# Biases loaded as rows, two weight slices in buffers of their own, two input tiles normalized early: a hybrid streaming-encoder layer on one core

## The chip, the cores and the metric

The kernel runs on 1 core of a Trainium2 chip. Its time is the device time of one launch in microseconds, the median over runs of the same build. A separate launch under the hardware profiler gives the trace; the trace's span is the time from the first to the last instruction of the core.

TensorE (PE) multiplies and transposes, VectorE (DVE), ScalarE (ACT) and GpSimd (POOL) work on tiles, SyncE (SP) issues the DMAs. TensorE's two granted clock levels are 1.2 and 2.4 GHz; the profile writes them as 0.5 and 1.0.

## The reference, cut to what matters

```
h = layer_norm(x, ln_in_g, ln_in_b)                     # x: 1024 x 1024
proj = h @ w_in + b_in                                  # 16 column groups
ya = gMLP spatial gating; yb = chunked band attention
yc = indexer (relu scores of iq, ik, iw), top-256 keys, attention over them
km, vm = split(mem @ w_mem_kv, 2)                       # mem: 256 x 1024, w_mem_kv: 1024 x 512
ym = attention of mq over km, vm
mixed = concat(ya*silu(a_g), yb*silu(b_g), yc*silu(c_g), ym*silu(m_g))
out = layer_norm(2**0.25 * h + mixed @ w_out + b_out, ln_g, ln_b)
```

All inputs and the output are float32. The change touches the loads and the order of work ahead of and in the first projections: layer_norm(x), the two biases ln_in_b and b_in, and mem @ w_mem_kv.

## The kernel before, in words

Sequence rows come in 8 tiles of 128 (`NB`); the model width is 8 blocks of 128 (`KT`). The input x is loaded as 8 tiles xt of 128 rows by 1024. `x_rows` normalizes one tile where it lies: two bn_stats, one bn_aggr and one subtract-and-multiply by g_in on VectorE, two tiny steps (add epsilon, power -0.5) on GpSimd (lines 134 and 135), one scaling by rs on ScalarE. The GpSimd and ScalarE steps carry a raised priority (`BOOST`).

`x_parts(half, ...)` turns four tiles: for each of the 8 column blocks TensorE makes 4 transposes into one PSUM bank (xT), ScalarE adds the bias column b_col and writes the high part hTh in a shortened format, VectorE writes what is left as hTl. So hT holds the normalized input, columns of the model on partitions, in two halves of 512 rows, each as a high and a low part.

`wblock` loads one slice of 128 columns of a weight matrix as one DMA into a raw buffer (there are 2, tag "raw"), and splits it in two pieces: ScalarE copies the high part, GpSimd (line 208) subtracts for the low part, into wblk tiles (tag "w", 5 buffers). `project` runs 24 matmuls a slice: for each of 8 blocks high times high, high times low, low times high. One projection of a narrow slice (72 columns: indexer key and indexer weights) has its parts in tiles named wnar; its slice is `wik`. `wmg` is the slice of the first memory gate. mem is turned by `mem_parts` into mT; `kv_of_mem` projects it with four slices of w_mem into km (slices 1 and 2) and vm (slices 3 and 4).

The order in the program is: x tiles 0 to 3, g_in, mem and two w_mem slices by `FIRST_LOADS`; the bias loads; mem turned; x tiles 0 to 3 normalized; km projected, with the loads of w_mem slices 3 and 4 in between (they take over the raw buffers of slices 1 and 2); x's first half turned; vm projected; wik and wmg loaded; the loads of x's tiles 4 to 7, on SyncE behind the fourth w_mem load (`loads[3]`); the first half of the wnar projection; tiles 4 to 7 normalized, on VectorE behind the last hTl of the first half (`first_half[0]`); the first half of the wmg projection; the second half turned; then the rest.

The program order is a priority: a planner with estimated durations and landing times decides the order in which each engine gets its instructions, and which buffer a tile takes. On the chip every engine runs its instructions in that order, each waiting for its inputs, so an instruction that waits holds back all behind it on its engine.

The biases are used as columns, one number a partition: b_col (8 columns) from ln_in_b, bias (31 columns, one for each 128-column group of the projection) from b_in, and hbias, half of bias. They are loaded with the partition as the fast index:

```
SP.dma_start(out=b_col, in_=ln_in_b.rearrange("(t p) -> p t", p=P))
SP.dma_start(out=bias[:m, a:a + n], in_=b_in[c0:c0 + n * m].rearrange("(t p) -> p t", p=m))
```

so each element is a piece of its own, 1024 in the first and 26 x 128 + 72 + 4 x 128 = 3912 in the three of bias.

Of the kernel before, what the change touches and what calls it, by code (L numbers as in the profile page):

```python
# [11 lines left out]
F32 = mybir.dt.float32  # L12
# [7 lines left out]
ALU = mybir.AluOpType  # L20
# [4 lines left out]
P = 128  # L25
NB = 8
KT = 8
# [46 lines left out]
def f32(ap):  # L74
    return ap.bitcast(F32)
# [3 lines left out]
def tile_trunk(ctx, tc, x, mem, ln_in_g, ln_in_b, w_in, b_in, a_ln_g, a_ln_b, a_ws, a_bs,  # L79
               b_rel_rev, t5_table, w_mem, w_out, b_out, ln_g, ln_b, bucket1h, out):  # L80
    nc = tc.nc
    G, SP = nc.gpsimd, nc.sync
# [20 lines left out]
    PE, V, S = Engine(nc.tensor), Engine(nc.vector), Engine(nc.scalar)  # L103

    def run(steps):

        while True:
            try:
                next(steps)
            except StopIteration as e:  # L110
                return e.value

    cp = ctx.enter_context(tc.tile_pool(name="cp", bufs=1))
    gp = ctx.enter_context(tc.tile_pool(name="gp", bufs=1))
# [4 lines left out]
    ident = cp.tile([P, P], F32, name="ident")  # L119
# [8 lines left out]
    def bcast(t, vec):  # L128
        n = vec.shape[-1]
        SP.dma_start(out=t, in_=bass.AP(tensor=vec.tensor, offset=vec.offset, ap=[[0, P], [1, n]]))  # L130
# [5 lines left out]


    col = {}
    bias = cp.tile([P, 31], F32, name="bias")
    hbias = cp.tile([P, 31], F32, name="hbias")  # L140
    spans = ((0, 26, P), (I_K, 1, 72), (M_Q, 4, P))
    for c0, n, _ in spans:
# [1 line left out]
            col[c0 + t * P] = len(col)  # L144

    def load_biases():
        V.memset(hbias, 0.0)
        for c0, n, m in spans:
            a = col[c0]
            SP.dma_start(out=bias[:m, a:a + n], in_=b_in[c0:c0 + n * m].rearrange("(t p) -> p t", p=m))  # L150
            V.tensor_scalar(hbias[:m, a:a + n], bias[:m, a:a + n], 0.5, None, ALU.mult)

    h_dram = [dp.tile([P, DM], F32, name=f"h_dram{r}") for r in range(NB)]

# [15 lines left out]
    def s4(name, dt=F32R, shape=(P, SEQ)):  # L170
        return gp.tile(list(shape), dt, tag="s4", bufs=S4, name=name)
# [11 lines left out]
    E = ep.enter_context(tc.tile_pool(name="ep", bufs=1))  # L183

    def ev(name, bufs=EV):
        return E.tile([P, 512], F32, tag="ev", bufs=bufs, name=name)

    def bank(tag, name=None):
        return ps.tile([P, 512], F32, tag=tag, bufs=BANKS[tag], name=name or tag)


    loads = []

    def wblock(w, c0, m=P):

        raw = E.tile([P, KT, P], F32, tag="raw", bufs=2, name="raw")
        loads.append(SP.dma_start(out=raw[:, :, :m], in_=w[:, c0:c0 + m].rearrange("(k p) c -> p k c", p=P)).ins)
        ts = []
        if m < P:
            narrow = [gp.tile([P, 2, KT // 2, m], F32R, tag=tag, bufs=1, name="wnar") for tag in ("planes", "score6")]  # L200
        for q in range(2):
            t = E.tile([P, 2, 4, P], F32R, tag="w", bufs=WB, name="wblk") if m == P else narrow[q]
            r = raw[:, 4 * q:4 * q + 4, :m]
            if WH[0] <= len(loads) < WH[1]:
                G.tensor_scalar(t[:, 0], r, 1.0, 0.0, ALU.mult, ALU.add)
            else:
                S.activation(t[:, 0], r, AF.Copy)
            G.tensor_sub(t[:, 1], r, f32(t[:, 0]))  # L208
            ts.append(t)
        return ts  # L210

    def project(t, a, b, m=P, hi=hh, lo=hl, tag="pp"):

        acc = bank(tag, "acc")
        for k in range(KT):
            wh, wl = t[k // 4][:, 0, k % 4, :m], t[k // 4][:, 1, k % 4, :m]
            PE.matmul(acc[:m, :b - a], wh, hi(k, a, b), start=(k == 0), stop=False)
            PE.matmul(acc[:m, :b - a], wh, lo(k, a, b), start=False, stop=False)
            PE.matmul(acc[:m, :b - a], wl, hi(k, a, b), start=False, stop=(k == KT - 1))
            yield  # L220
        return acc
# [56 lines left out]


    g_in = s4("g_in", F32)  # L280
    b_col = cp.tile([P, KT], F32, name="b_col")
    mT = [s4(f"mT{i}", F32R, (P, 4, 256)) for i in range(4)]

    def x_load(rb):
        tag = ("S", "S", "S", "S", "s4", "score7", "v3", "v3")[rb]
        xt = gp.tile([P, DM], F32, tag=tag, bufs={"S": SB, "v3": 2, "s4": S4}.get(tag, 1), name="xt")
        SP.dma_start(out=xt, in_=x[rb * P:(rb + 1) * P, :])
        return xt

    def x_rows(rb, xt):  # L290

        st = E.tile([P, 2, 6], F32, tag="st", bufs=2, name="st")
        V.bn_stats(st[:, 0], xt[:, :512])
        V.bn_stats(st[:, 1], xt[:, 512:])
        mv = E.tile([P, 2], F32, tag="mv", bufs=2, name="mv")
        V.bn_aggr(mv, st)
        rs = E.tile([P, 1], F32, tag="rs", bufs=2, name="rs")
        with tc.high_priority(offset=BOOST):
            rstd_of(mv[:, 1:2], rs)
        V.scalar_tensor_tensor(xt, xt, mv[:, 0:1], g_in, ALU.subtract, ALU.mult)  # L300
        with tc.high_priority(offset=BOOST):
            S.activation(xt, xt, AF.Copy, scale=rs)

    def x_parts(half, xts):

        high, rest = hT[half]
        for k in range(KT):
            pt = bank(("pt", "qk")[k % 2], "xT")
            for j in range(4):
                PE.transpose(pt[:, j * P:(j + 1) * P], xts[j][:, k * P:(k + 1) * P], ident)  # L310
            begin = S.activation(high[:, k, :], pt, AF.Identity, bias=b_col[:, k:k + 1])
            end = V.scalar_tensor_tensor(rest[:, k, :], pt, b_col[:, k:k + 1], f32(high[:, k, :]), ALU.add, ALU.subtract)
        return end.ins, begin.ins
# [6 lines left out]
    def mem_parts(r, mt):  # L320
        for q in range(2):
            pt = bank("pt")
            for j in range(4):
                k = 4 * q + j
                PE.transpose(pt[:, j * P:(j + 1) * P], mt[:, k * P:(k + 1) * P], ident)
            src, dst = pt.rearrange("p (a b) -> p a b", a=4), slice(r * P, (r + 1) * P)
            S.activation(mT[q][:, :, dst], src, AF.Copy)
            V.tensor_sub(mT[2 + q][:, :, dst], src, f32(mT[q][:, :, dst]))
# [29 lines left out]
    xts, mts, w_kv = [], [], []  # L358
    for what in FIRST_LOADS:
        if what == "x":  # L360
            xts.append(x_load(len(xts)))
        if what == "m":
            mts.append(mem_load(len(mts)))
        if what == "w":
            w_kv.append(wblock(w_mem, len(w_kv) * P))
        if what == "g":
            bcast(g_in, ln_in_g)
    SP.dma_start(out=b_col, in_=ln_in_b.rearrange("(t p) -> p t", p=P))
    load_biases()
    for r in range(2):  # L370
        mem_parts(r, mts[r])
    for rb in range(4):
        x_rows(rb, xts[rb])
    def kv_of_mem(i):

        t = ev("kv")
        for pair in range(2):
            acc = run(project(w_kv[2 * i + pair], 0, 256, P, mhi, mlo))
            S.activation(t[:, pair * 256:pair * 256 + 256], acc[:, :256], AF.Copy)
            if not i:  # L380
                w_kv.append(wblock(w_mem, 256 + pair * P))
        return t

    km = kv_of_mem(0)
    first_half = x_parts(0, xts)
    vm = kv_of_mem(1)


    wik = wblock(w_in, I_K, 72)
    wmg = wblock(w_in, M_G)  # L390
    ikh = s4("ikh")
# [3 lines left out]
    def ik_half(a, b):  # L395
        acc = run(project(wik, a, b, 72))
        bk = col[I_K]
        with tc.high_priority(offset=BOOST):
            for lo in (0, 64):
                S.activation(ikh[lo:lo + 64, a:b], acc[0:64, :], AF.Identity, bias=bias[0:64, bk:bk + 1])  # L400
            S.activation(iwT[64:72, a:b], acc[64:72, :], AF.Identity, bias=bias[64:72, bk:bk + 1])
            for lo in (0, 64):
                V.scalar_tensor_tensor(ikl[lo:lo + 64, a:b], acc[0:64, :], bias[0:64, bk:bk + 1],
                                       f32(ikh[0:64, a:b]), ALU.add, ALU.subtract)

    with tc.issue_after(loads[3]):
        xts += [x_load(rb) for rb in range(4, NB)]
    ik_half(0, 512)
    with tc.issue_after(first_half[0]):
        for rb in range(4, NB):  # L410
            x_rows(rb, xts[rb])
    run(gate_half(wmg, M_G, 6, 0, "pv"))
    second_half = x_parts(1, xts[4:])
# [390 lines left out]
    for g in range(4):  # L804
        SP.dma_start(out=bsT[64 * (g % 2):64 * (g % 2) + 64, g // 2, :],
                     in_=bass.AP(tensor=a_bs.tensor, offset=a_bs.offset + g * P, ap=[[0, 64], [1, P]]))
# [182 lines left out]
    for i, rb in enumerate(RBS):  # L989
        n = (rb + 1) * P  # L990
# [85 lines left out]
    for i, rb in enumerate(RBS):  # L1076
        n = (rb + 1) * P
# [241 lines left out]
    for k in range(KT):  # L1319
        hi, lo = [t[:, k % 4, :] for t in wo[k // 4]]  # L1320
        raw = E.tile([P, DM], F32, tag="raw", bufs=2, name="rawo")
        SP.dma_start(out=raw, in_=w_out[k * P:(k + 1) * P, :])
        for half in range(2):
            c = slice(half * 512, half * 512 + 512)
# [73 lines left out]
```

## Time and profile before

| | us |
|---|---|
| median of 3 runs | 672.88 (672.48 to 673.44) |
| profiled execution, device time | 671.02 |
| its span | 669.2 |
| TensorE busy | 633.7 (95%) |
| VectorE busy | 477.7 (71%) |
| ScalarE busy | 423.8 (63%) |
| GpSimd busy | 351.8 (53%) |

The mean granted TensorE clock over the span is 0.989. Busy times are sums over the whole span; an engine that is busy for a small share can still hold up another at one place. The chain that ended last is 68% TensorE; the first 50 us hold 13.7 us in which TensorE does not work (36.29 busy of 50), most of them before its first matmuls.

### The profile page before, as it was taken

What the parts mean: (1) busy time and instruction counts of PE and PEld (TensorE: products, weight loads), DVE (VectorE), ACT (ScalarE), POOL (GpSimd) and SP (SyncE); (2) the same over time, 40 slices, a digit from 0 to 9 for tenths busy, and PEclk for the clock granted to TensorE, in tenths of its full rate; (3) what the DMA queues carried; (4) which work ended last, traced back from release to release, by engine and by line L of the source; (5) the groups of instructions that cost most, each with busy time, mean ns of one, the idle gap of its engine ahead of it and who ended that gap; (6) DMA issues with size and microseconds to landing.
All of it is one profiled execution on the core that took longest, in us unless ns stands there. A gap on an engine that the chain in (4) does not pass through costs nothing.

```text
span 669.2 us, 11083 instructions
## 1 busy us (share of the span) xinstructions
PE 633.7 (95%) x3698; PEld 483.0 (72%) x3698; DVE 477.7 (71%) x1165; ACT 423.8 (63%) x947; POOL 351.8 (53%) x354
## 2 busy tenths in 40 slices
PE   4989999999999998988999999799999999999995
PEld 3867877767777777766677767577777777778785
DVE  6684254688866898898988889648658458877535
ACT  4665245576699888858999884446446666346210
POOL 3671320306346796574465645953224756557851
PEclk9999999999999999999999999899999999999998
DMA  9792511102234545255475534463102474225111
GB/s 283 239 328 84 169 54 28 35 18 81 62 111 111 126 119 133 51 129 134 109 131 107 147 83 85 96 136 110 38 12 83 141 247 132 90 82 188 64 63 64
DMA packets 121669, 75.30 MB, mean 113 GB/s; under 512 B 58976, under 2 KB 111500, under 8 KB 121612
## 3 DMA queue, kind: packets, MB, share of 16 engines
q1 hardware_dynamic: 121612, 74.59, 40.6%
q8 instruction: 29, 0.48, 0.3%
q14 instruction: 28, 0.23, 0.1%
HBM read 46.44 MB, written 17.64 MB: 96 GB/s over the span
## 4 chain that ended last, share of the span: by engine, by line
PE 68%; DVE 10%; ACT 9%; POOL 5%; issue 4%; DMA 2%; SPq 0%; POOLq 0%; DVEq 0%; ACTq 0%
PE acc L94 51%; PE qk L94 8%; PE pv L94 5%; ACT jka L94 4%; PE pt L94 3%; DVE jk L94 2%; ACT sc L94 1%; DMA xt<-in_x 1%; POOL wblk L208 1%; DMA pT<-sc 1%; DVE sc L94 1%; POOL rs L134 1%; POOL sc L546 1%; POOL sc L545 1%; PE xT L94 1%
## 5 line engine op out<-in xcount | busy, mean ns | idle before, releaser
L94 PE MATMUL acc<-hTh,wblk 128*128 128x512 f32 (+1 forms) x960 | 323.2, 401 | 2.2 <-ACT hTh L94 1.3
L94 PEld LDWEIGHTS acc<-hTh,wblk 128*128 128x128 f32 x960 | 178.3, 189 | 49.1 <-issue 8.9
L94 PE MATMUL acc<-hTl,wblk 128*128 128x512 f32 (+1 forms) x480 | 188.2, 392 | 0.0
L208 POOL TENSOR_TENSOR wblk<-raw,wblk 128x512 fp32r<-128x512 f32 x72 | 96.5, 1345 | 122.8 <-ACT wblk L94 119.9
L94 PEld LDWEIGHTS acc<-hTl,wblk 128*128 128x128 f32 x480 | 90.7, 189 | 17.6 <-issue 2.2
L94 ACT ACTIVATE jka<-score,cand 128x768 int8<-128x768 f32 (+2 forms) x93 | 96.5, 1038 | 8.7 <-DVE cand L94 8.1
L94 PEld LDWEIGHTS <-pT 128*128 128x128 f16 x656 | 46.2, 99 | 32.5 <-issue 21.7
L546 POOL TENSOR_TENSOR sc<-sc 128x512 f16<-128x512 f32 (+4 forms) x48 | 58.7, 1229 | 2.7
L94 PE MATMUL pv<-v,pT 128*128 128x192 bf16 (+1 forms) x528 | 55.3, 238 | 4.9 <-DMA pT<-sc 3.2
L94 DVE SCALAR_TENSOR_TENSOR score<-relu,iw,score 128x384 f32<-128x384 f32 (+5 forms) x42 | 42.7, 1039 | 18.4 <-ACT relu L94 16.4
L94 ACT ACTIVATE wblk<-raw 128x512 fp32r<-128x512 f32 x72 | 44.4, 626 | 17.2 <-PE acc L94 8.6
L94 PE MATMUL acc<-woh,mh 128*128 128x512 f32 (+1 forms) x144 | 55.2, 383 | 0.0
L94 PE MATMUL acc<-wol,mh 128*128 128x512 f32 (+1 forms) x144 | 53.6, 372 | 0.0
L94 PE MATMUL acc<-woh,ml 128*128 128x512 f32 (+1 forms) x144 | 53.6, 373 | 0.0
L94 ACT ACTIVATE relu<-qk 128x384 f32<-128x384 f32 (+2 forms) x80 | 35.5, 532 | 22.5 <-PE qk L94 22.4
L545 POOL TENSOR_SCALAR sc<-sc 128x512 f16<-128x512 f32 (+4 forms) x48 | 31.4, 658 | 34.5 <-ACT sc L94 28.9
L94 ACT ACTIVATE sc<-sc,nb 128x640 f32<-128x640 f32 (+7 forms) x64 | 46.5, 729 | 1.0
L94 ACT ACTIVATE o<-o,ri 128x64 f32<-128x64 f32 x96 | 28.1, 342 | 25.8 <-DVE o L94 25.7
L94 ACT ACTIVATE pT<-pt 128x512 f16<-128x512 f32 (+3 forms) x48 | 22.2, 485 | 28.0 <-PE pt L94 27.9
L94 DVE TENSOR_SCALAR_CACHE_REDUCE jk<-planes,lo 128x384 bf16<-128x384 uint16 (+2 forms) x48 | 35.7, 743 | 1.0
L94 DVE TENSOR_SCALAR_CACHE_REDUCE jk<-planes,cand 128x384 bf16<-128x384 bf16 (+2 forms) x45 | 33.5, 743 | 1.1
L94 DVE TENSOR_REDUCE o<-pv 128x128 f32<-128x384 f32 x48 | 26.3, 549 | 9.8 <-PE pv L94 9.7
(204 smaller groups left out, 1224.8 us busy)
## 6 DMA issues: line engine op xcount, KB each, us to landing
raw<-in_w_in SPq DMA_DIRECT2D x32, 512.0 KB, 3.8
xt<-in_x SPq DMA_DIRECT2D x8, 512.0 KB, 4.8
h_dram<-xt SPq DMA_DIRECT2D x8, 512.0 KB, 5.6
gate<-t SPq DMA_DIRECT2D x16, 256.0 KB, 2.1
rawo<-in_w_out SPq DMA_DIRECT2D x8, 512.0 KB, 4.7
hr<-h_dram SPq DMA_DIRECT2D x8, 512.0 KB, 5.3
out<-hr SPq DMA_DIRECT2D x7, 512.0 KB, 2.6
gate<-gate SPq DMA_DIRECT2D x48, 64.0 KB, 2.0
```

Source lines behind the costliest of these rows:

```text
L94: ins = op(*a, **k)
L134: G.tensor_scalar(tmp, var, EPS, 0.0, ALU.add, ALU.add)
L208: G.tensor_sub(t[:, 1], r, f32(t[:, 0]))
L545: G.tensor_scalar(high, sc[:, :n], 1.0, 0.0, ALU.mult, ALU.add)
L546: G.tensor_sub(rest, sc[:, :n], high)
```

## The change

Biases: the 8 rows of ln_in_b and the 31 of b_in are loaded as rows of up to 128 contiguous numbers into one tile of 39 partitions (cleared first), turned by one TensorE transpose, and copied from PSUM into one tile `cols`, of which b_col and bias are the first 8 and the last 31 columns. hbias is made from all of bias in one instruction. The transpose stands behind `mem_parts` in the program.

w_mem slices 3 and 4: each is loaded as two DMAs of half the rows into tiles with tags that nothing else uses at that time ("jk", "vt", twice "near"), and before km is projected in the program.

x's second half: its four loads follow the w_mem loads at once, and only tiles 6 and 7 are normalized behind the first half's last hTl on VectorE; tiles 4 and 5 are free of that.

```diff
-    bias = cp.tile([P, 31], F32, name="bias")
+    cols = cp.tile([P, KT + 31], F32, name="cols")
+    b_col, bias = cols[:, :KT], cols[:, KT:]
...
     def load_biases():
-        V.memset(hbias, 0.0)
+
+        rows = ev("rows")[:KT + 31, :P]
+        V.memset(rows, 0.0)
+        SP.dma_start(out=rows[:KT], in_=ln_in_b.rearrange("(t p) -> t p", p=P))
         for c0, n, m in spans:
-            a = col[c0]
-            SP.dma_start(out=bias[:m, a:a + n], in_=b_in[c0:c0 + n * m].rearrange("(t p) -> p t", p=m))
-            V.tensor_scalar(hbias[:m, a:a + n], bias[:m, a:a + n], 0.5, None, ALU.mult)
+            a = KT + col[c0]
+            SP.dma_start(out=rows[a:a + n, :m], in_=b_in[c0:c0 + n * m].rearrange("(t p) -> t p", p=m))
+        return rows
+
+    def turn_biases(rows):
+
+        pt = bank("pv", "bT")
+        n = KT + 31
+        PE.transpose(pt[:, :n], rows, ident[:n, :n])
+        V.tensor_copy(cols, pt[:, :n])
+        V.tensor_scalar(hbias, bias, 0.5, None, ALU.mult)
...
-    def wblock(w, c0, m=P):
-
-        raw = E.tile([P, KT, P], F32, tag="raw", bufs=2, name="raw")
-        loads.append(SP.dma_start(out=raw[:, :, :m], in_=w[:, c0:c0 + m].rearrange("(k p) c -> p k c", p=P)).ins)
+    def wblock(w, c0, m=P, places=None):
+
+        src = w[:, c0:c0 + m].rearrange("(k p) c -> p k c", p=P)
+        if places:
+            raws = [gp.tile([P, 4, P], F32, tag=tag, bufs=bufs, name="raw") for tag, bufs in places]
+            for q in range(2):
+                loads.append(SP.dma_start(out=raws[q], in_=src[:, 4 * q:4 * q + 4]).ins)
+        else:
+            raw = E.tile([P, KT, P], F32, tag="raw", bufs=2, name="raw")
+            loads.append(SP.dma_start(out=raw[:, :, :m], in_=src).ins)
+            raws = [raw[:, 4 * q:4 * q + 4, :m] for q in range(2)]
...
-    b_col = cp.tile([P, KT], F32, name="b_col")
...
-    SP.dma_start(out=b_col, in_=ln_in_b.rearrange("(t p) -> p t", p=P))
-    load_biases()
+    rows = load_biases()
     for r in range(2):
         mem_parts(r, mts[r])
+    turn_biases(rows)
...
             S.activation(t[:, pair * 256:pair * 256 + 256], acc[:, :256], AF.Copy)
-            if not i:
-                w_kv.append(wblock(w_mem, 256 + pair * P))
         return t
 
+    for pair in range(2):
+        w_kv.append(wblock(w_mem, 256 + pair * P, places=((("jk", 1), ("vt", 1)), (("near", 2), ("near", 2)))[pair]))
+    xts += [x_load(rb) for rb in range(4, NB)]
     km = kv_of_mem(0)
...
-    with tc.issue_after(loads[3]):
-        xts += [x_load(rb) for rb in range(4, NB)]
     ik_half(0, 512)
-    with tc.issue_after(first_half[0]):
-        for rb in range(4, NB):
+    for rb in range(4, NB):
+        with tc.issue_after(first_half[0]) if rb > 5 else ExitStack():
             x_rows(rb, xts[rb])
```

## Rows read from the trace of the kernel before

**Rows 1.** The page, busy us, share of the span and instructions of each engine.

```profile
PE 633.7 (95%) x3698; PEld 483.0 (72%) x3698; DVE 477.7 (71%) x1165; ACT 423.8 (63%) x947; POOL 351.8 (53%) x354
```

**Rows 2.** TensorE in order of time: start, us, operation, count, idle before and releaser.

```profile
15.04 2.24 PE L94 MATMUL acc<-mT,wblk 128*128 128x256 f32 x11 [0.88 <-POOL wblk L208]
...
32.49 0.45 PE L94 MATMUL acc<-hTh,wnar 128*72 128x512 f32 x1 [1.37 <-ACT wnar L94]
...
44.12 1.25 PE L94 MATMUL xT<-ident,xt 128*128 128x128 f32 x10
46.45 0.76 PE L94 MATMUL xT<-ident,xt 128*128 128x128 f32 x5 [1.07 <-ACT xt L94]
47.49 0.77 PE L94 MATMUL xT<-ident,xt 128*128 128x128 f32 x5 [0.28 <-ACT xt L94]
...
49.74 0.50 PE L94 MATMUL acc<-hTh,wblk 128*128 128x512 f32 x1 [1.26 <-ACT hTh L94]
```

**Rows 3.** SyncE's queue in order of time, same columns; a time covers the issues counted.

```profile
10.42 0.43 SPq L368 DMA_DIRECT2D b_col<-in_ln_in_b  x1
10.89 5.91 SPq L150 DMA_DIRECT2D bias<-in_b_in  x3
...
17.46 3.33 SPq L197 DMA_DIRECT2D raw<-in_w_mem_kv  x2
20.84 1.99 SPq L287 DMA_DIRECT2D xt<-in_x  x4
24.77 9.72 SPq L197 DMA_DIRECT2D raw<-in_w_in  x3
```

**Rows 4.** Busy us by stretch: PE, PEld, DVE, ACT, POOL, clock, DMA share, GB/s.

```profile
14.00:15.00 1.00, 0.16 (x2) 0.00 (x0) 1.00 (x3) 1.00 (x2) 1.00 (x2) 1.00 1.05 400
...
16.00:17.00 1.00, 1.00 (x7) 1.00 (x6) 1.00 (x1) 0.00 (x0) 1.00 (x2) 0.50 1.31 7
```

**Rows 5.** ScalarE in order of time.

```profile
33.38 1.15 ACT L94 ACTIVATE wblk<-raw 128x512 fp32r<-128x512 f32 x2 [0.60 <-DMA raw<-in_w_in]
...
45.25 2.19 ACT L94 ACTIVATE xt<-xt,rs 128x1024 f32<-128x1024 f32 x2 [0.91 <-POOL rs L135]
...
49.00 3.00 ACT L94 ACTIVATE hTh<-xT,b_col 128x512 fp32r<-128x512 f32 x5
```

**Rows 6.** VectorE in order of time.

```profile
18.43 0.47 DVE L94 TENSOR_SCALAR hbias<-bias 128x26 f32<-128x26 f32 x3
...
26.22 3.39 DVE L94 SCALAR_TENSOR_TENSOR hTl<-xT,b_col,hTh 128x512 fp32r<-128x512 f32 x5 [4.75 <-ACT hTh L94]
...
32.72 2.46 DVE L94 BATCH_NORM_STATS2 st<-xt 128x6 f32<-128x512 f32 x4
...
44.72 1.49 DVE L94 SCALAR_TENSOR_TENSOR ikl<-acc,bias,ikh 64x512 fp32r<-64x512 f32 x2
```

**Rows 7.** Busy us in stretches of 5 us, columns as in the stretches above.

```profile
5.00:10.00 5.00, 2.08 (x10) 2.00 (x10) 2.83 (x5) 1.82 (x3) 0.80 (x2) 1.00 1.00 376
...
15.00:20.00 5.00, 4.96 (x29) 4.96 (x30) 4.92 (x10) 1.02 (x3) 5.00 (x5) 0.66 0.86 67
...
45.00:50.00 5.00, 2.39 (x17) 1.66 (x16) 2.50 (x5) 4.75 (x7) 1.80 (x4) 1.00 1.07 395
...
425.00:430.00 5.00, 2.63 (x16) 1.98 (x15) 2.68 (x4) 0.00 (x0) 5.00 (x5) 0.86 0.40 78
430.00:435.00 5.00, 4.18 (x26) 3.15 (x24) 2.21 (x9) 2.35 (x6) 3.43 (x4) 0.50 0.64 117
```

**Rows 8.** GpSimd in order of time.

```profile
25.17 2.55 POOL L208 TENSOR_TENSOR wblk<-raw,wblk 128x512 fp32r<-128x512 f32 x2 [0.43 <-ACT wblk L94]
...
36.60 1.37 POOL L134 TENSOR_SCALAR rs<-mv 128x1 f32<-128x1 f32 x2
37.94 1.08 POOL L135 TENSOR_TENSOR rs<-rs,mhalf 128x1 f32<-128x1 f32 x2
```

**Rows 9.** DMA issues of the first 70 us: engine, count, size, median us to landing.

```profile
bias<-in_b_in SPq DMA_DIRECT2D x1, 2.0 KB, 2.3
```

More of the change, by code (lines that the diff above doesn't have):

```diff
@@ L202, in wblock @@
             t = E.tile([P, 2, 4, P], F32R, tag="w", bufs=WB, name="wblk") if m == P else narrow[q]
-            r = raw[:, 4 * q:4 * q + 4, :m]
+            r = raws[q]
             if WH[0] <= len(loads) < WH[1]:
```

## The prediction

> **What bounds the kernel now.** The page's busy times come first: TensorE works 633.7 us of a span of 669.2 us, so at most some 35 us can be won by letting it wait less [rows 1]. The kernel's arithmetic does not change; what the edits can move is when TensorE is fed. So I read TensorE's own order of time in the first 50 us and looked at the entries with an idle time behind them [rows 2]. After the start-up (the matmul at 15.04 is the last that waits there) it runs without a gap until it stands 1.37 us before 32.49, the first matmul of the indexer-key projection (wnar). It runs on to the transposes of x's second half at 44.12, and there it stands 1.07, 0.28 and 1.26 us. That is 3.98 us of waits; all else in this stretch is work.
>
> Next, why those waits. On SyncE's queue the four bias loads are issued from 10.42 to 16.80 us, the last three taking 5.91 us; the third and fourth w_mem slices come only from 17.46, x's tiles 4 to 7 from 20.84, w_in's first slices from 24.77 [rows 3]. The DMA engines moved 400 GB/s from 14 to 15 us and 7 GB/s from 16 to 17 us with a share above 1: that is the bias transfer, element by element [rows 4]. ScalarE still waits 0.60 us for a slice of w_in at 33.38 [rows 5]. VectorE stands 4.75 us before 26.22 and then normalizes tiles 4 to 7 from 32.72 to 44.72 in one solid piece of 12.0 us, 3.0 us a tile [rows 6]. So x's second half is late because its four normalizations start only when the first half is turned, and wnar is late because its weights come, and are split, last.
>
> **The change part by part.**
>
> *Biases as rows.* 1024 elements of b_col and 3912 of bias are now moved one by one; they become 39 rows of 288 or 512 bytes. SyncE's issue falls from 0.43 + 5.91 = 6.34 us [rows 3] to four issues of some 0.43, 1.7 us: 4.6 us of queue, and the nearly empty stretch of the DMA engines goes. TensorE has work during it, so by itself this gains nothing. The price is one transpose, one copy out of PSUM and one multiply. VectorE's three multiplies took 0.47 us [rows 6]; the copy and one multiply I take at the same, bounds −0.2 to +0.4. Ten transposes in a row take 1.25 us [rows 2], 0.125 each, and twice that at the half clock that the row of 16 to 17 us shows [rows 4]. With a wait of its own I charge **+0.3 us** to TensorE, bounds 0.1 and, if it stands in front of its data, the second rival. Queued behind it are the memory projections, and behind the copy on VectorE the normalizations of tiles 2 and 3.
>
> *Own buffers for two slices.* The w_mem slices 3 and 4 no longer wait for the two raw buffers, so the loads of x's second half, of wik and of wmg stand behind transfer time alone. Tile 3 is in between 15 and 16 us by the fall of the rate [rows 4]; I take 15.3. Then 3.15 MB (two slices in four halves, four tiles) at the 376 GB/s of 5 to 10 us [rows 7] are 8.4 us: tile 7 is in at 23.7, wik and wmg, 0.82 MB more, at 26, against 33.4 now. ScalarE works 1.02 us of the 5 from 15 to 20 us [rows 7], so the third slice's split has room there and wik's after it. The projection's first step needs only the first turned tile, long there, so the wait goes: **−1.37 us**, bounds 0 (ScalarE still splits wik after its last hTh) and −1.37. Late next is wmg, needed 24 matmuls on; it has 7 us to spare.
>
> The Trainium skill, in "DMA: Bandwidth & Descriptors", section Bandwidth, asks for transfers of at least 1 MiB and so speaks against cutting each slice into two of 256 KB. The row of 5 to 10 us shows 376 GB/s with 512 KB transfers queued together, so the trace does not bear it out for a full queue.
>
> *Two tiles normalized early.* Tiles 4 and 5 lose their place behind the first half: 2 × 3.0 = 6.0 us of VectorE go into the 4.75 us before 26.22 [rows 6]. The 1.25 us that do not fit push hTl. Its last tile is read by the eighth step of the wnar projection, some 5 us after the first, and that hides it; without this cover it costs 1.25. Tiles 6 and 7 then start at 32.72 + 1.25 = 34.0 and take 6.0 us: 40.0. GpSimd's two small steps add 0.69 + 0.54 [rows 8] and ScalarE's scaling 1.10, half of the 2.19 for two [rows 5]: 42.3 us. TensorE is through with the wnar and first wmg projections at 44.12 − 1.37 = 42.75. So 1.07 and 0.28 go, with 0.4 us of margin; of the 1.26 before the first hTh I keep half, since the gate's two activations still stand ahead of it on ScalarE. **−2.0 us** of the 2.61, bounds 0 and −2.61.
>
> These two tiles also bring GpSimd's steps, 1.37 + 1.08 = 2.45 us a pair, into a stretch where GpSimd splits the w_mem slices, with a gap of 0.43 us before the last [rows 8]. They are boosted, so the last split can come up to 2.0 us late, and TensorE reads it at once. Bounds 0 (other transposes or wnar fill in) and +2.0; I take **+0.3**, nearer to zero, because from 25 us on TensorE has other work to be given.
>
> *The sum.* −1.37 − 2.0 + 0.3 + 0.3 = −2.8 us. The profiled execution took 671.02 us (its span and 1.8 around it), so 668.2; the median of the runs, 672.88, lies 1.9 above that execution, so **670.1**. TensorE works 95% of the span [rows 1], and what follows the first 50 us starts from its results there, so the shift should pass on.
>
> A second rule speaks of the clock. From 44.12 to 49.74 TensorE did nothing but transposes and waiting [rows 2], and the granted clock of 45 to 50 us is 1.00, the 2.4 GHz level [rows 7]; so moved transposes are charged no clock. The Trainium skill, in "TensorE: Matmul & The Clock Gate", Part 4, says that a transpose does not count as busy for the clock; by that the stretch should have dropped, and here it did not.
>
> **The rivals.**
>
> 1. *Given back later.* From 425 to 430 us TensorE works 2.63 us of 5, and from 430 to 435 at 0.50 of its clock, while GpSimd works 5.00 of 5 [rows 7]. The plan orders everything by estimated times, so a shift at 50 us can change what stands there. If that place, or one like it, takes up what was won: 672.9, no change. For: from 425 on it is not TensorE that sets the pace. Against: what sets it also started from earlier results. The reverse is as open: 2.4 us of idle and some 2 us lost to the low clock vanish in whole or half, 665.7 to 667.9.
>
> 2. *Slower: the turned biases stand in the way.* The rows lie in the queue behind tile 3, in by 16 us at the latest; the last old bias load landed 2.3 us after its issue [rows 9]. So they are there at 17.5 to 18.3. If the plan puts the transpose straight after those of mem (12.5 us), TensorE stands until 18.3 where its group now starts at 15.04 [rows 2]: 3.3 us, and 0.8 for the few matmuls before that, 4.1. VectorE's copy holds tiles 2 and 3 as long, which takes the turning of the first half out of the cover of the projections: eight evictions at 0.60, 4.8 us (five took 3.00 [rows 5]), of which I count 2. 6.1 lost against 3.4 gained: 675.6. It decides from 3.4 us lost. Against it: the plan put the old multiplies at 18.43, just where their data were in [rows 6].
>
> 3. *Only half.* If VectorE's pieces run slower among GpSimd's and tiles 6 and 7 end at 43.3, the waits at 46 to 50 shrink by 1.0 instead of 2.0: 671.1.
>
> 4. *Transfers that do not overlap.* If each of the eight loads behind tile 3 paid the 2.3 us of [rows 9] on top of its bytes, tile 7 would be in at 15.3 + 18.4 + 8.4 = 42.1 and wik at 45; wnar would start 13 us late, 686. The 376 GB/s of queued transfers speak against it. By the fit for a single transfer in the Trainium skill ("DMA: Bandwidth & Descriptors", section Anatomy of one DMA), the eight would take an estimated 23 us.
>
> **Chances.** Forecast 0.48, within 668.5 to 671.5; rival 1 with no change 0.16, its reverse 0.10; rival 2 0.11; rival 3 0.12; rival 4 0.03. A measurement of this kernel tells 0.2% (1.35 us) from no change, so faster is below 671.5: forecast, reverse and most of rival 3, 0.67. Within: the first rival and the mild end of the second, 0.20. Slower: 0.13. The range, 666.0 to 674.2, leaves out the fourth rival, the full price of the second and the far end of the reverse.
>
> **What would show it.** Right: the wait before the first wnar matmul is gone, and the second half's transposes start near 42 us with under 1 us of waiting; VectorE's idle before the first hTl is under 1.5 us; the DMA engines move above 300 GB/s from 16 to 24 us. Wrong: TensorE waits on the rows' DMA before 19 us (second rival), or on GpSimd's split near 27 us, or 45 to 50 us looks as before. If the shift is there at 60 us and the end is not earlier, the loss lies behind it.

## The result, and the profile after

The changed kernel takes 676.43 us (675.33 to 676.64), the kernel before, timed beside it, 672.68 (671.33 to 673.44): a ratio of 1.0063 [1.0048, 1.0077], 0.6% slower. The forecast was 670.1. The profiled execution took 675.33 us with a span of 673.5, against 671.02 and 669.2. The work is the same: TensorE's busy time, where it was 633.7 [rows 1], reads

```profile
PE 637.2 (95%) x3699; PEld 484.5 (72%) x3699; DVE 475.5 (71%) x1164; ACT 423.5 (63%) x947; POOL 351.8 (52%) x354
```

First question: where in the span does the time go? A mark that both kernels pass is VectorE's first copy of the scores into planes, with which the long search begins (start, us, engine, operation, count). Before:

```profile
178.51 0.35 DVE L94 COPY planes<-score 128x384 bf16<-128x384 bf16 x1
```

After:

```profile
183.45 0.35 DVE L94 COPY planes<-score 128x384 bf16<-128x384 bf16 x1
```

It is 4.94 us late, more than the whole loss of span (4.3). From the mark to the end it is 669.2 − 178.51 = 490.7 us before and 490.1 after. So nothing is lost or won behind the mark, and the loss lies ahead of it. TensorE's order of time in the changed kernel has all the new waits between 30 and 53 us (idle before and releaser in brackets; the rows answer to [rows 2]):

```profile
32.28 0.98 PE L94 MATMUL xT<-ident,xt 128*128 128x128 f32 x5 [1.56 <-DVE hTl L94]
33.59 1.22 PE L94 MATMUL xT<-ident,xt 128*128 128x128 f32 x7 [0.33 <-DVE hTl L94]
34.87 0.45 PE L94 MATMUL acc<-hTh,wnar 128*72 128x512 f32 x1
...
48.13 0.77 PE L94 MATMUL xT<-ident,xt 128*128 128x128 f32 x5 [0.81 <-ACT xt L94]
49.17 0.77 PE L94 MATMUL xT<-ident,xt 128*128 128x128 f32 x5 [0.27 <-ACT xt L94]
...
52.77 0.41 PE L94 MATMUL vt<-ident,kv 128*128 128x128 f32 x2 [2.84 <-ACT v3m L94]
```

The wait of 1.37 us on wnar is gone, as foreseen, but the row itself begins at 34.87 instead of 32.49: two waits on hTl, 1.89 us, came in its place. The three waits of the second half were 2.61 us and are 3.92. From 30 to 60 us TensorE works 25.88 us before and 23.99 after, and the granted clock falls:

```profile
30.00:60.00 30.00, 23.99 (x111) 16.46 (x111) 18.54 (x28) 20.30 (x35) 13.00 (x14) 0.94 0.60 211
```

What came as foreseen is the load side. SyncE issues all four bias loads in 1.25 us, where it took 6.34 [rows 3], and x's second half is issued by 18.3 us:

```profile
10.54 0.35 SPq L151 DMA_DIRECT2D rows<-in_ln_in_b  x1
10.94 0.90 SPq L154 DMA_DIRECT2D rows<-in_b_in  x3
...
16.41 1.93 SPq L305 DMA_DIRECT2D xt<-in_x  x4
```

The DMA engines move 326 GB/s from 15 to 20 us, where they moved 67 [rows 7], and 366 in the next 5 (columns as there, the last two DMA share and GB/s):

```profile
15.00:20.00 5.00, 4.99 (x29) 4.99 (x30) 3.45 (x5) 1.65 (x4) 5.00 (x5) 0.66 1.15 326
20.00:25.00 5.00, 5.00 (x43) 4.82 (x42) 4.33 (x9) 3.31 (x6) 4.87 (x5) 1.00 1.03 366
```

So the data are early and the results late. GpSimd's order of time shows why. L134 and L135 are the two small steps of a tile; the split is L208 in the kernel before and L227 in the changed one (the experiments' kernels shift these numbers a little). Before, tile 3 above and tiles 6 and 7 below:

```profile
20.36 1.20 POOL L134 TENSOR_SCALAR rs<-mv 128x1 f32<-128x1 f32 x1
21.64 0.57 POOL L135 TENSOR_TENSOR rs<-rs,mhalf 128x1 f32<-128x1 f32 x1
22.18 2.56 POOL L208 TENSOR_TENSOR wblk<-raw,wblk 128x512 fp32r<-128x512 f32 x2
...
39.30 3.22 POOL L208 TENSOR_TENSOR wblk<-raw,wblk 128x512 fp32r<-128x512 f32 x2 [0.27 <-ACT wblk L94]
42.49 1.20 POOL L134 TENSOR_SCALAR rs<-mv 128x1 f32<-128x1 f32 x1
```

After:

```profile
21.60 0.23 POOL L134 TENSOR_SCALAR rs<-mv 128x1 f32<-128x1 f32 x1
21.96 3.32 POOL L227 TENSOR_TENSOR wblk<-raw,wblk 128x512 fp32r<-128x512 f32 x2
25.23 0.57 POOL L135 TENSOR_TENSOR rs<-rs,mhalf 128x1 f32<-128x1 f32 x1
...
41.63 4.38 POOL L227 TENSOR_TENSOR wblk<-raw,wblk 128x512 fp32r<-128x512 f32 x2 [2.66 <-ACT wblk L94]
45.99 0.39 POOL L134 TENSOR_SCALAR rs<-mv 128x1 f32<-128x1 f32 x2
46.35 1.07 POOL L135 TENSOR_TENSOR rs<-rs,mhalf 128x1 f32<-128x1 f32 x2
```

Between the two small steps of tile 3 (21.60 and 25.23) now stand two pieces of a w_mem slice, 3.32 us. Before, the power step stood straight behind the first step, and the next split came after it. Further on, the two steps of tiles 6 and 7 wait behind the split of the first indexer-query slice (iq0), 4.38 us. VectorE had their variances at 41.48:

```profile
20.57 0.20 DVE L94 COPY cols<-bT 128x39 f32<-128x39 f32 x1 [2.08 <-PE bT L94]
...
29.25 0.75 DVE L94 SCALAR_TENSOR_TENSOR hTl<-xT,cols,hTh 128x512 fp32r<-128x512 f32 x1 [0.31 <-ACT hTh L94]
...
41.08 0.40 DVE L94 BATCH_NORM_AGGREGATE mv<-st 128x2 f32<-128x12 f32 x2
```

and behind GpSimd stands ScalarE, 1.84 us for tile 3 and 4.86 for tiles 6 and 7, with the evictions of the indexer key, the gate's activations and all hTh of the second half in line behind it:

```profile
25.83 1.16 ACT L94 ACTIVATE xt<-xt,rs 128x1024 f32<-128x1024 f32 x1 [1.84 <-POOL rs L135]
...
28.53 0.69 ACT L94 ACTIVATE hTh<-xT,cols 128x512 fp32r<-128x512 f32 x1 [1.15 <-PE xT L94]
...
46.93 2.19 ACT L94 ACTIVATE xt<-xt,rs 128x1024 f32<-128x1024 f32 x2 [4.86 <-POOL rs L135]
49.02 1.36 ACT L94 ACTIVATE ikh<-acc,cols 64x512 fp32r<-64x512 f32 x2
...
52.54 3.01 ACT L94 ACTIVATE hTh<-xT,cols 128x512 fp32r<-128x512 f32 x5
```

Before, ScalarE scaled tile 3 and wrote the first hTh at

```profile
22.40 1.14 ACT L94 ACTIVATE xt<-xt,rs 128x1024 f32<-128x1024 f32 x1
...
25.52 2.99 ACT L94 ACTIVATE hTh<-xT,b_col 128x512 fp32r<-128x512 f32 x5
```

and the second half's first hTh at 49.00 [rows 5]: the changed kernel is 3.4, 3.0 and 3.5 us late.

The split of iq0 stood ahead of the steps of tiles 6 and 7 before as well, but at 39.30 to 42.5, 0.9 us past their variances, which were there at 41.61. Now its slice comes later: it takes over the raw buffer of wik, whose split ended at 34.1 before and ends at 36.46 now, since wik's pieces are behind the late hTh on ScalarE.

The reading to be tested: GpSimd now has long splits in its order just where short steps that others wait for become ready, those of w_mem because they land earlier, that of iq0 because it lands later, while tiles 6 and 7 are ready when they were before. The rival, theory A: the turned biases hold VectorE (2.08 us in the row at 20.57) and with it tile 3.

### The profile page after: what moved, and what is told of

Its sections match the earlier page's. It is cut to its first block, busy times and chain, and to the rows that moved or that the text cites. A ratio compares the mean times of both kernels' runs of the same rounds, so it can differ in the third digit from the quotient of the medians.

```text
span 673.5 us, 11088 instructions
## 1 busy us (share of the span) xinstructions
PE 637.2 (95%) x3699; PEld 484.5 (72%) x3699; DVE 475.5 (71%) x1164; ACT 423.5 (63%) x947; POOL 351.8 (52%) x354
## 4 chain that ended last, share of the span: by engine, by line
PE 52%; ACT 15%; DVE 14%; POOL 7%; issue 6%; DMA 4%; SPq 1%; POOLq 0%; DVEq 0%; ACTq 0%
PE acc L94 38%; PE qk L94 7%; ACT jka L94 6%; PE pv L94 4%; DVE jk L94 3%; PE pt L94 2%; ACT sc L94 2%; DVE sc L94 1%; POOL wblk L227 1%; DMA raw<-in_w_in 1%; DVE thr L94 1%; DMA xt<-in_x 1%; POOL sc L563 1%; DMA hr<-h_dram 1%; ACT wblk L94 1%
## 5 line engine op out<-in xcount | busy, mean ns | idle before, releaser
L227 POOL TENSOR_TENSOR wblk<-raw,wblk 128x512 fp32r<-128x512 f32 x72 | 99.9, 1392 | 130.1 <-ACT wblk L94 127.1
```

## The experiments

Ratios are to the kernel before on the same chip, with the 95% interval; its medians beside these runs were 672.24, 672.26 and 672.16 us.

**One part alone.** Three kernels keep one part each and undo the two others. Undone means: the four loads element by element; `wblock` without places, at its old position, with x's second half behind `loads[3]`; or

```diff
-        with tc.issue_after(first_half[0]) if rb > 5 else ExitStack():
+        with tc.issue_after(first_half[0]) if rb > 3 else ExitStack():
```

Only the biases as rows:

> The kernel before with the biases as turned rows alone; old buffers, old load order, tiles 4 to 7 all normalized behind the first half. Theory A (the copy of the turned biases stands in VectorE's order ahead of tile 3 and waits for a TensorE that runs at half clock there): VectorE waits some 2 us for the transpose near 18 to 20 us, the first hTh starts 1 to 3 us later than 25.5, and the time is 1 to 4 us over before. Theory B (the turn costs little; the loss comes from GpSimd, whose small steps for tiles 6 and 7 stand behind the split of a weight slice that lands late): within 1.3 us of before.

Only the own buffers:

> The kernel before with the two w_mem slices in buffers of their own and x's last four loads right behind them; biases element by element as before, tiles 4 to 7 all normalized behind the first half. Theory A: no loss at the start, within 1.3 us of before or up to 2 us faster. Theory B: the next slice of w_in is still loaded only when wnar's raw buffer is free, its split is planned ahead of GpSimd's steps for tiles 6 and 7, and the second half comes 3 to 5 us late: 2 to 5 us slower than before.

Only tiles 4 and 5 free:

> The kernel before with tiles 4 and 5 free of the first half; old biases, old buffers, old load order. Theory A: tiles 4 and 5 land near 26 us or later, so little moves: within 1.5 us of before. Theory C (the boosted pieces of tiles 4 and 5 push the first half's evictions): the last hTh ends 1 to 3 us later than 32.0 and the time is 1 to 3 us over before.

Measured: 671.93 us, 0.9993 [0.9983, 1.0003]; 672.69, 1.0003 [0.9995, 1.0012]; 671.04, 0.9981 [0.9972, 0.9990]. No part costs anything by itself, and the early tiles alone win 0.2%. The loss is made by parts together. That the own buffers alone would cost 2 to 5 us, through the split of iq0, has not come true. Theory A's condition came true with rows only, VectorE waited 3.15 us for the turned biases at 21.61, but the loss it was to bring did not.

**The turn placed later.** All of the change, with the turn behind the four normalizations in the program:

```diff
-    turn_biases(rows)
     for rb in range(4):
         x_rows(rb, xts[rb])
+    turn_biases(rows)
```

> The changed kernel with the transpose and copy of the biases placed behind the four normalizations of x's first half in the program. Theory A: VectorE's wait of 2.1 us ahead of tile 3 goes, the first hTh starts 2 to 3 us earlier than the 28.5 of the changed kernel, and the time falls by 2 to 4 us. Theory B: the start is earlier, but GpSimd's steps for tiles 6 and 7 stay behind the split near 46 us and the time falls by less than 1.3 us.

Measured: 676.07 us, 1.0056 [1.0042, 1.0069]. The plan put the copy into the same place on VectorE, where it waited 3.04 us, and every order of GpSimd, ScalarE and VectorE is that of the changed kernel, so this says nothing on theory A.

**GpSimd's order in the second half, VectorE's order in the first.** The first kernel keeps the split of iq0 behind the power step of tile 7 (`pows` collects these steps in `rstd_of`):

```diff
-    iqs = [iq_tile(0)]
+    with tc.issue_after(pows[-1]):
+        iqs = [iq_tile(0)]
```

> The changed kernel with one order changed: GpSimd's split of the first indexer-query slice stands behind the two small steps of x tile 7 instead of ahead of those of tiles 6 and 7. TensorE, ScalarE and VectorE keep the changed kernel's order. Theory B (head of line on GpSimd): the steps run near 42 instead of 46 us, ScalarE's wait of 4.9 us ahead of the scaling of tile 6 shrinks to under 1, the first index matmul comes 2 to 4 us earlier than its 80.9, and the time falls by 2 to 4 us against the changed kernel. Theory A: only the copy of the biases matters; less than 1 us.

The second tests theory A: the bias copy stands behind the centring of tile 3 on VectorE.

```diff
-        x_rows(rb, xts[rb])
+        centred = x_rows(rb, xts[rb])
+    with tc.issue_after(centred):
+        turn_biases(rows)
```

> The changed kernel with one order changed: VectorE's copy of the turned biases stands behind the centring of x tile 3, two instructions later. TensorE and ScalarE keep the changed kernel's order. Theory A: VectorE's wait of 2.1 us no longer holds tile 3, the first hTh comes 1 to 3 us earlier than 28.5, and 2 to 4 us of the time come back. Theory B: the first half is up to 2 us earlier, but GpSimd's order at 41 to 46 us is as it was and less than 1.3 us come back, unless the weight slice behind it lands that much earlier too.

The third has both orders:

> Both reorderings together, on VectorE and on GpSimd. If the two waits add, 4 to 6 us come back against the changed kernel and the time is 0 to 2 us under before; if they are one chain, no more than the better of the two alone.

Measured: 673.82 us, 1.0021 [1.0008, 1.0034]; 677.08, 1.0080 [1.0065, 1.0096]; 673.65, 1.0026 [1.0010, 1.0043]. GpSimd's order for tiles 6 and 7 is worth 676.43 − 673.82 = 2.6 us; up to the mark the order of the other engines is that of the changed kernel. There the small steps follow the variances and the split comes third (GpSimd, then ScalarE, whose wait was 4.86; under 1 was expected):

```profile
41.58 1.34 POOL L136 TENSOR_SCALAR rs<-mv 128x1 f32<-128x1 f32 x2 [2.39 <-DVE mv L94]
...
44.95 2.54 POOL L229 TENSOR_TENSOR wblk<-raw,wblk 128x512 fp32r<-128x512 f32 x2
```

```profile
44.49 2.20 ACT L94 ACTIVATE xt<-xt,rs 128x1024 f32<-128x1024 f32 x2 [2.05 <-POOL rs L137]
```

The third kernel gains no more than the first. Theory A falls. With the copy out of the way VectorE centres tile 3 at 18.87 instead of 21.59:

```profile
18.87 1.28 DVE L94 SCALAR_TENSOR_TENSOR xt<-xt,mv,g_in 128x1024 f32<-128x1024 f32 x1
```

but GpSimd still splits first, and the power step and with it the scaling come later than in the changed kernel, not earlier:

```profile
22.70 3.62 POOL L227 TENSOR_TENSOR wblk<-raw,wblk 128x512 fp32r<-128x512 f32 x2
26.29 1.54 POOL L135 TENSOR_TENSOR rs<-rs,mhalf 128x1 f32<-128x1 f32 x1
```

The 2.08 us of VectorE's wait were a wait beside the one that counts. That holds with GpSimd's first-half order as it is here; no run moves the copy in a kernel where that order is mended.

**Two parts together.** Rows and early tiles:

> Biases as rows and tiles 4 and 5 free of the first half, without the early loads of the w_mem slices and of x. Theory B wants the early loads for the loss: within 1.5 us of before. If the copy and the early tiles are enough together, 2 to 4 us over before.

Own buffers and early tiles:

> Own buffers with early loads, and tiles 4 and 5 early, with the biases element by element as before. If the biases as rows have no part in the loss, 2 to 5 us over before; if the loss needs the rows (which let the w_mem slices land 5 us earlier), within 1.5 us of before.

Rows and own buffers:

> Biases as rows and own buffers with early loads, all of tiles 4 to 7 behind the first half. If the early w_mem splits on GpSimd are the cause alone, 2 to 5 us over before; if tiles 4 and 5 have to come in among them, within 1.5 us of before.

Measured: 670.83 us, 0.9981 [0.9969, 0.9992]; 674.02, 1.0029 [1.0017, 1.0041]; 676.51, 1.0080 [1.0062, 1.0098]. The own buffers do no harm alone and harm in both pairs. With rows and own buffers both orders are bad: the power step of tile 3 comes at 25.29 behind 3.32 us of splits, and ScalarE stands 4.86 us before tile 4 at 44.21. With own buffers and early tiles, 1.9 us over the kernel before and so between its two forecasts, the second is (ScalarE stands 4.98 us before 44.28), and the first in part, with one piece of a split between the steps and the power step at 23.93. With the own buffers alone the first is bad in the same part: the power step is 2.4 us and the first hTh, at 26.64, 1.1 us later than before. The late split is cut in two by the small steps:

```profile
22.77 1.29 POOL L217 TENSOR_TENSOR wblk<-raw,wblk 128x512 fp32r<-128x512 f32 x1
24.02 0.57 POOL L135 TENSOR_TENSOR rs<-rs,mhalf 128x1 f32<-128x1 f32 x1
...
37.87 1.29 POOL L217 TENSOR_TENSOR wblk<-raw,wblk 128x512 fp32r<-128x512 f32 x1 [2.27 <-ACT wblk L94]
39.13 1.38 POOL L134 TENSOR_SCALAR rs<-mv 128x1 f32<-128x1 f32 x2
40.47 1.29 POOL L217 TENSOR_TENSOR wblk<-raw,wblk 128x512 fp32r<-128x512 f32 x1
```

So a late small step is not a loss by itself. The pair of rows and early tiles, which is faster than the kernel before, shows it best: its split of iq0 stands ahead of the steps of tiles 6 and 7 too, and these start 4.5 us past their variances (39.41), as in the changed kernel (41.48 and 45.99). But ScalarE waits only 0.71 us for them, because its order has the indexer key's evictions ahead of these scalings (GpSimd, then ScalarE):

```profile
40.30 3.65 POOL L227 TENSOR_TENSOR wblk<-raw,wblk 128x512 fp32r<-128x512 f32 x2 [1.24 <-ACT wblk L94]
43.92 0.39 POOL L134 TENSOR_SCALAR rs<-mv 128x1 f32<-128x1 f32 x2
```

```profile
41.69 1.36 ACT L94 ACTIVATE ikh<-acc,cols 64x512 fp32r<-64x512 f32 x2
...
44.87 2.19 ACT L94 ACTIVATE xt<-xt,rs 128x1024 f32<-128x1024 f32 x2 [0.71 <-POOL rs L135]
```

In the changed kernel these evictions stand behind the scalings (49.02 and 46.93), and ScalarE does nothing meanwhile, though the projection that they evict had ended at 44.55. What GpSimd's late steps cost in the second half thus depends on ScalarE's order too. No run changes that order by itself.

**GpSimd's order in the first half, and both.** All of the change, with w_mem slices 3 and 4 split behind the power step of tile 3:

```diff
     for pair in range(2):
-        w_kv.append(wblock(w_mem, 256 + pair * P, places=...))
+        with tc.issue_after(pows[3]):
+            w_kv.append(wblock(w_mem, 256 + pair * P, places=...))
```

> The changed kernel with GpSimd's splits of w_mem slices 3 and 4 ordered behind the power step of x tile 3 (in the changed kernel it stood behind two or three of them). Theory B1 (GpSimd's order sets the first half too): the scaling of tile 3 comes near 23 instead of 25.8 us, the first hTh near 26 instead of 28.5, the first index matmul 2 to 4 us before its 80.9, and 1.5 to 4 us of the time come back. Rival (TensorE then waits for the split slices instead): under 1 us comes back.

And with the order of iq0 as well:

> Both GpSimd orders at once: w_mem's splits behind tile 3's power step, the first indexer-query split behind tile 7's. If the two GpSimd waits are the whole loss, 4 to 6 us come back and the time is 0 to 2 us under before. If the second wait only follows from the first, no more than the better of the two alone (2.6 us for the second).

Measured: 672.48 us, 1.0008 [0.9995, 1.0021], and 670.03, 0.9963 [0.9946, 0.9979]. The first order alone is worth 676.43 − 672.48 = 4.0 us, both 6.4. The edge stands on GpSimd alone, but from 23.6 us on the planner gave the other engines a new order as well: TensorE turns the second group of x's blocks behind 12 of the memory matmuls instead of 36, and VectorE has the first hTl ahead of tile 5's centring. So 4.0 and 6.4 us are what the edge and the plan that follows from it are worth together; only the 2.6 us above are GpSimd's order alone. The version with both orders beats both kernels: 0.4% under the kernel before, 1.0% under the changed one. GpSimd now does the small steps when their inputs are there:

```profile
22.42 0.57 POOL L137 TENSOR_TENSOR rs<-rs,mhalf 128x1 f32<-128x1 f32 x1
22.96 6.03 POOL L229 TENSOR_TENSOR wblk<-raw,wblk 128x512 fp32r<-128x512 f32 x4
...
38.08 1.34 POOL L136 TENSOR_SCALAR rs<-mv 128x1 f32<-128x1 f32 x2 [1.83 <-DVE mv L94]
...
41.45 2.55 POOL L229 TENSOR_TENSOR wblk<-raw,wblk 128x512 fp32r<-128x512 f32 x2
```

TensorE's only waits from 25 to 60 us are then these two, 1.45 us together, and the search starts at 178.28, 5.2 us before that of the changed kernel:

```profile
47.49 0.51 PE L94 MATMUL acc<-hTh,wblk 128*128 128x512 f32 x1 [1.16 <-ACT hTh L94]
...
48.72 0.63 PE L94 MATMUL xT<-ident,xt 128*128 128x128 f32 x4 [0.29 <-DVE hTl L94]
```

One thing stays unwon: the clock.

```profile
50.00:55.00 5.00, 5.00 (x20) 3.82 (x19) 2.96 (x5) 2.42 (x6) 2.60 (x3) 0.73 0.31 111
```

5.00 × (1 − 0.73) = 1.35 us are lost in this stretch, none in the kernel before, whose granted clock there is 1.00.

## Why the prediction was wrong

The step that failed is the one on GpSimd: "a stretch where GpSimd splits the w_mem slices ... I take +0.3, nearer to zero, because from 25 us on TensorE has other work to be given". The two orders of GpSimd, with the orders that the plan made of them elsewhere, cost 6.4 us, by the last kernel against the changed one. I priced how late the steps of tiles 4 and 5 would make a split, and not the other direction, how late a split would make the steps: slices of w_mem that land earlier are also planned earlier, ahead of tile 3's second step, and the split of iq0, which stood ahead of the steps of tiles 6 and 7 all along, now runs when these are ready. Bounds of 0 and +2.0 for this were bounds on the wrong victim. The rest of the forecast, point by point:

- *Own buffers, −1.37.* The loads came as worked out. The wait on wnar is gone in the changed kernel, but two on hTl (1.89 us) stand where it was, because the first hTh is 3.0 us late. In the version with both orders TensorE has no wait before 47.49, so the wait is gone there without another in its place.
- *Early tiles, −2.0.* In the changed kernel they bring +1.31 (3.92 − 2.61). VectorE's idle time before the first hTl did shrink, from 4.75 to 0.31 as foreseen; but tiles 6 and 7 began at 38.71, not 34.0, since hTl came late, and their last step waited on GpSimd. With both orders the second half's transposes start at 43.74 (42.75 was forecast), and 1.45 us of the 2.61 stay, where some 0.6 were to stay.
- *Biases, +0.3.* TensorE's transpose, at 20.28, took 0.25 us without a wait. VectorE waited 2.08 us for it, which is half of the second rival; with rows only VectorE waits 3.15 us and nothing is lost, and the kernel with the copy moved behind tile 3 gains nothing, so that rival is refuted as the cause. With both GpSimd orders GpSimd stands 0.59 us for tile 3's variance, behind that copy; whether this costs anything is not tested.
- *The clock, charged nothing.* After the 2.84 us wait the granted clock of 53.1 to 56.5 us is 0.50, the 1.2 GHz level, and from 30 to 60 us some 1.15 us are lost to it (busy time times what the clock lacks, 5 us stretch by stretch). In the version with both orders it falls too, to 0.50 from 49.3 to 52.7 us, after 3.75 us (43.74 to 47.49) of nothing but transposes and 1.16 us of waiting, and then 1.8 us of matmuls and four transposes; before, 5.6 us of transposes and waiting kept 1.00 [rows 2, 7]. So my sentence "moved transposes are charged no clock" was drawn from one case that did not repeat. The Trainium skill, in "TensorE: Matmul & The Clock Gate", Part 4, says a transpose does not count as busy as a matmul does; the fall in the version with both orders is in line with that, the kernel before is not, and what decides between the two is left open.
- *Rival 1 (given back later)* is refuted by the mark: from it to the end it is 489.8 to 491.7 us in all 14 kernels. *Rival 3 (only half)* has its mechanism in the trace, not the loss: VectorE centred tiles 6 and 7 in 3.46 us beside the split (from 41.40) and in 2.43 us where the split came later (from 41.61, with GpSimd's second order). *Rival 4 (transfers that do not overlap)* is refuted by the 326 and 366 GB/s: these 10 us moved 3.5 MB, more than its eight loads hold (3.15), where its fit, one for transfers that GpSimd issues while these are SyncE's, gave 23 us. The Trainium skill, "DMA: Bandwidth & Descriptors", section Bandwidth, asks for 1 MiB a transfer; halves of 256 KB queued among tiles of 512 KB moved at these rates.
- *The sum.* The forecast's 670.1 us is what the version with both orders takes (670.03). By what it is made up of that is partly luck: 0.8 us of waits more than were to stay and 1.6 us of clock (30 to 60 us, worked out as above) were not in the sum.

Of the 4.94 us at the mark, 1.89 are more idle time of TensorE from 30 to 60 us and 1.15 the clock. The last 1.9 are busy time too: up to the first indexer matmul (at 76.06 before and 80.93 after) TensorE is busy 61.70 and 64.70 us for the same matmuls and the one transpose of the biases, with the clock's share in that; more closely I have not broken it down. That the two orders of GpSimd, with the plan that follows from them, win all of it back is shown by the version with both, whose search starts 0.2 us ahead of the kernel before's. Of the 2.1 us that it wins by the medians its trace shows only those 0.2: the kernel before was profiled in an execution (671.02) 1.1 us under its median beside this version (672.16), the version in one (670.81) 0.8 us over its own.

## What to carry to other kernels

An edit that makes a load land earlier also moves the work that waits for it, on every engine that takes its instructions in a planned order: for each such piece, look which short instruction of that engine may now stand behind it, who waits for that one, and whether that engine has other work ahead of it in its own order. A 0.6 us step that releases a row tile belongs ahead of a 2.5 us split where the next engine would stand idle for it, and it is cheap to say so in the program with one ordering edge. When parts are harmless alone and costly together, pairs of parts and the position of one instruction on its engine tell more than the busy shares, which hardly moved here.

## What the runs showed of the hardware

Wide GpSimd pieces beside VectorE's wide ones took longer: the same 128x512 split is 1.27 us a piece in the rows at 44.95 and 41.45 (two in 2.54 and 2.55) and 2.19 in the changed kernel's row at 41.63 (two in 4.38), while VectorE centred two tiles in the 3.46 us from 41.40. So a split ahead of a small step costs the more when VectorE is busy; that the overlap is the cause was not tested by itself.

Some executions ran their first matmuls more slowly than others though the granted-clock column shows 1.00 in both. In the profiled execution of the kernel with rows only, the lone matmul that takes 0.39 us in the changed kernel's took

```profile
12.63 0.58 PE L94 MATMUL acc<-mT,wblk 128*128 128x256 f32 x1
```

and the column stays at 1.00 there from 10 to 25 us, while the changed kernel's reads 0.66 from 15 to 20. The eleven matmuls from 15 us took 2.72 and 2.28 us. I take it that the column lacks a record in such executions. Their traces hold some 1 us more up to 20 us (the transpose of the biases stands at 21.32 instead of 20.28); which of the executions behind the medians were of this kind is not known.
